# Expert layer of a decoder trunk: activations fetched by row transfers through slot tables in DRAM

## The chip, the cores and the metric

The kernel runs on one NeuronCore of one Trainium2 chip. The metric is the device time of one execution in microseconds (us), and for the kernel before it is 1563.54 us, the median of 3 runs that lie between 1563.01 and 1564.38 us. TensorE is called PE, VectorE DVE, ScalarE ACT, GpSimd Pool, and SP is the engine that issues the weight transfers. Everything is float32. A product of full precision is made of three TensorE products of rounded halves: each operand is split into a high part (rounded, made by ACT) and a low part (the rest, made by DVE).

## The reference, cut to what matters

A sequence of 16 meta tokens and 256 tokens of width 1024 passes two layers. The change touches the last part, the mixture of 8 experts of the second layer:

```python
logits = h @ w_router                                   # 256 tokens x 8 experts
top_val, top_idx = lax.top_k(logits, 2)
gates = softmax(top_val)                                # one weight per chosen expert
combine = sum(one_hot(top_idx, 8) * gates[..., None], axis=-2)
for e in range(8):
    y = y + combine[..., e:e+1] * ((silu(h @ w_gate[e]) * (h @ w_up[e])) @ w_down[e])
```

Here `h` is the normed residual, the three matrices of an expert are 1024 x 3584, 1024 x 3584 and 3584 x 1024, and the result is added to the residual.

## The kernel before, in words

Each expert works on up to 128 tokens, its slots. `pos` holds for each token and expert the slot that the token would have there, `sel` is 1 where the token chose the expert, `comb` holds the gates (lines 823 to 857 and 1028 to 1036). If an expert has more than 128 tokens, a loop under `tc.If(over == 1)` does the rest at the end; the data of these runs do not enter it.

**Gathering.** `gather` (L870) brings the activations of two experts together, as columns of a matrix `xh`, `xl` (high and low part, 1024 features by 2 x 128 slots). DVE builds a one-hot matrix `pg` from `pos` and `sel` (L875), and PE multiplies the token rows `h_hi` and `h_lo` by it: for each of 8 feature blocks 4 matmuls of 256 columns (L882), and 4 products of one column for the row scale `rsl`. ACT copies each block out of PSUM twice, into `xh` and `xl` (L883, L884). There is one buffer for `xh` and one for `xl`. The gather of pair 0 runs before the experts, and those of pairs 1, 2 and 3 are hung into the list of work near the end of experts 1, 3 and 5 (L1049).

**The expert loop.** `run` (L921) goes through a flat list of slabs. An expert has NJ = 7 steps j, and a step has three weight tiles of 2 MiB: gate, up and down. A tile is loaded by SP into one of 6 staging slots in turn (`wload`, L139 to L145; 5 in pool `wst`, 1 in `wst2`) and cut in two units of 2048 columns. A unit is split by ACT (`whi`, L163) and DVE (`wlo`, L164) into one of 3 buffers, and serves 12 matmuls of 512 columns. So a step has 72 such matmuls. Between them, 4 transposes turn the step's hidden activations (`turn_h`, L975), and the down product of a step follows the gate and up products of the next step. The products of `down` add up in two PSUM banks `dn` over all 7 steps.

**Scattering.** After an expert, `scatter` (L893), hung into step 1 of the next one (L1051), splits the two `dn` banks by ACT and DVE, turns the one-hot matrix by 2 transposes, multiplies by it in 8 matmuls of 512 columns (L907, L908) and adds 4 results, scaled by the gate, to the residual `acc` (L909). The last expert's `scatter` ends with the stores of the output.

**Order.** The program is written for a planner. It takes instructions in program order as priority, simulates the engines in time, and fixes each engine's order. `tc.high_priority(offset=PRI)` puts a block ahead by 300 places. A hook such as `hooks[e, "g", 1, 3]` runs a function behind a given slab: expert, which of gate, up, down, step, quarter of the tile.

**The dense layer.** The first layer's feed-forward (L581 to L625) is the place of one added part. There Pool multiplies `sg` by `rs` once for each of 28 blocks of 128 columns (L613), and DVE takes its result for the next product (L614). `psmm` has 4 PSUM banks in turn, and a block takes two of them. Just ahead of it Pool adds up the squares of 8 blocks (`sqa`, L193) while DVE makes the low parts `a_lo` (L199).

Of the kernel before, what the change touches and what calls it, by code (L numbers as in the profile page):

```python
# [18 lines left out]
P = 128  # L19
# [62 lines left out]
HIL = 3  # L82
UNIT = 2048

TCARGS = dict(schedule_with_timeline_sim=True)
# [13 lines left out]
def build(nc, tc, ctx, A, out, dbg=None, upto=None):  # L99
# [10 lines left out]
    hil = ch.enter_context(tc.tile_pool(name="hil", bufs=HIL))  # L110
    ps = ctx.enter_context(tc.tile_pool(name="ps", bufs=1, space=PSUM))

    def psmm():
# [5 lines left out]
    def pstr():  # L119
        return ps.tile([P, 512], F32, name="tr", bufs=2)  # L120
# [460 lines left out]
    with ExitStack() as c2:  # L581
        pf = c2.enter_context(tc.tile_pool(name="pf", bufs=2, reuse_waits="tile"))
        NJF = FF // 512

        def dense_down(j, fh, fl):
# [202 lines left out]
    acc = late.tile([P, 2, D], F32, name="acc")  # L788
    h_hi = late.tile([P, 2, D], F32R, name="h_hi")
    h_lo = late.tile([P, 2, D], F32R, name="h_lo")  # L790
    wst2 = ctx.enter_context(tc.tile_pool(name="wst2", bufs=WST2, side="right", reuse_waits="tile"))
    stage["pools"] = [wst] * WST + [wst2] * WST2
    cg_ = ctx.enter_context(ExitStack())
    hgp = cg_.enter_context(tc.tile_pool(name="hgp", bufs=1, side="right", reuse_waits="tile"))
# [38 lines left out]
    m8 = late.tile([P, 2, 8], F32, name="m8")  # L833
    m2 = hgp.tile([P, 2, 8], F32, name="m2")
    rep = hgp.tile([P, 2, NE], F32, name="rep")
    ex = late.tile([P, 2, NE], F32, name="ex")
# [29 lines left out]
    with ExitStack() as c4:  # L866
        pe = c4.enter_context(tc.tile_pool(name="pe", bufs=1, reuse_waits="tile"))
        wk = c4.enter_context(tc.tile_pool(name="wke", bufs=2, reuse_waits="tile"))

        def gather(es, xh, xl, pos=pos, sel=sel):  # L870

            pg = wk.tile([P, 2, 256], F32R, name="pg", bufs=2)
            for t in range(2):
                for i, e in enumerate(es):
                    nc.vector.tensor_scalar(pg[:, t, i * P:(i + 1) * P], iota, pos[:, t, e:e + 1],  # L875
                                            sel[:, t, e:e + 1], op0=OP.is_equal, op1=OP.mult)
            n = len(es) * P
# [12 lines left out]
            nc.vector.tensor_copy(r[:, :len(es)], o[:, :len(es)])  # L890
            return pg, r

        def scatter(e, col, yps, pg, comb=comb, post=None):  # L893

            y = stage["hil"].tile([P, UNIT], F32R, name="whi")
            yh, yl = y[:, 0:D], y[:, D:2 * D]
            pt = pstr()
            for t in range(2):
                tr(pt[:, t * P:(t + 1) * P], f(pg[:, t, col * P:(col + 1) * P]), P)
            pT = wk.tile([P, 256], F32R, name="pT2", bufs=1)  # L900
            nc.scalar.copy(pT, pt[:, :256])
            for n in range(2):
                sl = slice(n * 512, (n + 1) * 512)
                split_ps(yh[:, sl], yl[:, sl], yps[n])
                for t in range(2):
# [5 lines left out]
                    if post:  # L911
                        post(t, sl)

        def store(t, sl=slice(0, D)):
# [110 lines left out]

        gather_pair(0)

# [7 lines left out]
        for t in range(2):  # L1035
            nc.vector.tensor_scalar(comb[:, t], ex[:, t], dn[:, 1, t:t + 1], None, op0=OP.mult)
        o = psdn()
        mm(o[:, 0:NE], oneb, selb[:, 0], True, False)
# [3 lines left out]
        nc.vector.tensor_scalar(ovf, mx[:, 0:1], float(P), None, op0=OP.is_gt)  # L1042

        over = nc.values_load(ovf[0:1, 0:1], min_val=0, max_val=1)
# [12 lines left out]
        with tc.If(over == 1):  # L1057
# [6 lines left out]
            with tc.For_i(0, NE, 1) as e:  # L1064
                xh = wk.tile([P, KT, 256], F32R, name="xh", bufs=1)
                xl = wk.tile([P, KT, 256], F32R, name="xl", bufs=1)
                pg, r = gather((0,), xh, xl, cur[:, 0], cur[:, 1])
                ws = [w[bass.ds(e, 1)].rearrange("o a b -> (o a) b") for w in (WG, WU, WD)]
# [3 lines left out]
                run(more)  # L1072
                scatter(0, 0, st["y"], pg, cur[:, 2])
                nc.vector.tensor_copy(nxt[:, :, :, 0:NE - 1], cur[:, :, :, 1:NE])
# [26 lines left out]
```

## Time and profile before

| what | value |
|---|---|
| median of the runs (3 runs) | 1563.54 us |
| profiled execution, its own time | 1562.15 us |
| its span in the profile | 1560.4 us |
| PE busy | 1526.8 us, 98% |
| DVE busy | 1232.8 us, 79% |
| ACT busy | 1033.1 us, 66% |
| Pool busy | 118.3 us, 8% |
| moved by DMA | 433.70 MB, mean 278 GB/s |
| chain that ended last | PE 93%, ACT 3%, DVE 2% |

The span goes from the first to the last instruction, and the time of the execution is 1.75 us longer. Busy time counts each engine by itself; matmuls overlap in the pipeline, so the time from one matmul's start to the next one's is shorter than its duration. The chain of waits is followed back from the last instruction, and it is merged into pieces of one engine and line. The expert stage takes the last 1000 us, from about 559 us on.

### The profile page before, as it was taken

To read this page: it belongs to the slowest core of one execution; us is meant where nothing else is said; L and a number is where in the kernel's file an instruction comes from. 1 tells how busy PE (TensorE), PEld (TensorE's weight loads), DVE (VectorE), ACT (ScalarE), POOL (GpSimd) and SP (SyncE) were. 2 spreads that over 40 slices of the span, in tenths; PEclk is the share of its full clock that TensorE was granted. 3 is DMA by queue.
4 is the path that set the end of the run, shared out by engine and by line. 5 is a ranking of instruction groups with operands and counts; after the bars stand their busy time and mean duration, and the time that the engine had idled before them with its cause. 6 is when DMAs were issued, how large, how long until landed. Compare 5 with 4: busy or idle time off the path is not lost.

```text
span 1560.4 us, 21288 instructions
## 1 busy us (share of the span) xinstructions
PE 1526.8 (98%) x8558; PEld 1335.6 (86%) x8558; DVE 1232.8 (79%) x1248; ACT 1033.1 (66%) x1116; POOL 118.3 (8%) x146
## 2 busy tenths in 40 slices
PE   7989999999999989999999999999999999999997
PEld 7978999999999978888888888888888888888885
DVE  6875766666765678889879889879888888988986
ACT  5686644444545687767777777777777777777774
POOL 4431211112300100000000000000000000000000
PEclk9999999999999999999999999999999999999999
DMA  9521544443743659999999999998999998999980
GB/s 318 188 108 34 184 162 163 162 163 131 257 162 109 221 185 377 369 361 345 376 341 333 373 377 337 372 338 326 391 355 343 372 365 314 377 359 363 357 320 29
DMA packets 165822, 433.70 MB, mean 278 GB/s; under 512 B 5917, under 2 KB 10693, under 8 KB 158549
## 3 DMA queue, kind: packets, MB, share of 16 engines
q1 hardware_dynamic: 165652, 432.20, 75.4%
q8 instruction: 69, 1.13, 0.3%
q14 instruction: 37, 0.30, 0.1%
q10 hardware_dynamic: 64, 0.07, 0.0%
HBM read 431.21 MB, written 1.05 MB: 277 GB/s over the span
## 4 chain that ended last, share of the span: by engine, by line
PE 93%; ACT 3%; DVE 2%; issue 1%; DMA 0%; SPq 0%; DVEq 0%; ACTq 0%
PE mm L129 62%; PE dn L129 24%; PE tr L129 5%; PE tr L132 2%; ACT whi L163 1%; DVE wlo L164 1%; DMA w<-in_dsa_w_in_dram 0%; ACT kz L433 0%; DVE wlo L222 0%; ACT junk L298 0%; PE mm L132 0%; DVE sc L383 0%; ACT vz L475 0%; DVE acc L909 0%; DVE m L382 0%
## 5 line engine op out<-in xcount | busy, mean ns | idle before, releaser
L164 DVE TENSOR_TENSOR wlo<-w,whi 128x2048 fp32r<-128x2048 f32 (+1 forms) x473 | 930.4, 1981 | 179.0 <-ACT whi L163 177.5
L163 ACT CAST whi<-w 128x2048 fp32r<-128x2048 f32 (+1 forms) x473 | 781.5, 1658 | 401.9 <-PE mm L129 256.7
L129 PE MATMUL mm<-whi,xh 128*128 128x512 f32 x896 | 353.8, 395 | 1.2 <-ACT xl L884 1.0
L129 PE MATMUL mm<-wlo,xh 128*128 128x512 f32 x896 | 354.2, 397 | 0.4 <-DVE wlo L164 0.4
L129 PE MATMUL mm<-whi,xl 128*128 128x512 f32 x896 | 352.7, 394 | 0.0
L129 PEld LDWEIGHTS mm<-wlo,xh 128*128 128x128 f32 x896 | 169.1, 189 | 39.3 <-DVE wlo L164 3.6
L129 PE MATMUL mm<-a_hi,whi 128*128 128x272 f32 (+2 forms) x688 | 199.0, 291 | 2.8 <-ACT whi L221 1.4
L129 PEld LDWEIGHTS mm<-whi,xh 128*128 128x128 f32 x896 | 169.2, 189 | 37.3 <-ACT xl L884 1.2
L129 PEld LDWEIGHTS mm<-whi,xl 128*128 128x128 f32 x896 | 169.0, 189 | 37.1
L129 PE MATMUL mm<-a_hi,wlo 128*128 128x272 f32 (+2 forms) x688 | 198.7, 290 | 0.7 <-DVE wlo L164 0.7
L129 PE MATMUL mm<-a_lo,whi 128*128 128x272 f32 (+2 forms) x688 | 198.6, 289 | 0.0
L129 PE MATMUL dn<-whi,hTl 128*128 128x512 f32 x448 | 174.8, 391 | 1.4 <-DVE hTl L169 1.4
L129 PE MATMUL dn<-whi,hTh 128*128 128x512 f32 x448 | 174.3, 391 | 0.0
L129 PE MATMUL dn<-wlo,hTh 128*128 128x512 f32 x448 | 159.5, 396 | 0.3
L129 PEld LDWEIGHTS mm<-a_hi,whi 128*128 128x128 f32 (+1 forms) x688 | 128.5, 187 | 3.9 <-ACT whi L221 1.6
L129 PEld LDWEIGHTS mm<-a_hi,wlo 128*128 128x128 f32 (+1 forms) x688 | 128.4, 187 | 1.9 <-DVE wlo L164 0.9
L129 PEld LDWEIGHTS mm<-a_lo,whi 128*128 128x128 f32 (+1 forms) x688 | 128.7, 187 | 0.6
L129 PEld LDWEIGHTS dn<-whi,hTl 128*128 128x128 f32 x448 | 84.1, 188 | 20.0 <-DVE hTl L169 1.8
L129 PEld LDWEIGHTS dn<-whi,hTh 128*128 128x128 f32 x448 | 84.1, 188 | 18.3
L129 PEld LDWEIGHTS dn<-wlo,hTh 128*128 128x128 f32 x448 | 82.2, 188 | 19.3 <-DVE wlo L164 3.3
L129 PE MATMUL mm<-b_hi,whi 128*128 128x272 f32 (+1 forms) x264 | 75.1, 292 | 2.8 <-DVE gp L661 1.4
L129 PE MATMUL mm<-b_lo,whi 128*128 128x272 f32 (+1 forms) x264 | 75.8, 289 | 0.0
(350 smaller groups left out, 1676.1 us busy)
## 6 DMA issues: line engine op xcount, KB each, us to landing
w<-in_moe_w_gate_dram SPq DMA_DIRECT2D x56, 2048.0 KB, 10.1
w<-in_moe_w_up_dram SPq DMA_DIRECT2D x56, 2048.0 KB, 9.8
w<-in_moe_w_down_dram SPq DMA_DIRECT2D x56, 2048.0 KB, 9.0
w<-in_ffn_w_gate_dram SPq DMA_DIRECT2D x7, 2048.0 KB, 10.1
w<-in_ffn_w_up_dram SPq DMA_DIRECT2D x7, 2048.0 KB, 7.9
w<-in_ffn_w_down_dram SPq DMA_DIRECT2D x7, 2048.0 KB, 7.8
w<-in_mlstm_w_in_dram SPq DMA_DIRECT2D x6, 2048.0 KB, 10.3
w<-in_dsa_w_in_dram SPq DMA_DIRECT2D x4, 2048.0 KB, 10.2
```

The source lines that it names most:

```text
L129: nc.tensor.matmul(o, l, r, start=start, stop=stop)
L132: nc.tensor.transpose(o, i, ident[:k, :k])
L163: nc.scalar.copy(hr, src)
L164: nc.vector.tensor_tensor(lr, src, f(hr), OP.subtract)
```

## The change

- Two tables are set up in DRAM: `xs` with 256 rows for each expert (128 slots and 128 for the overflow), each a token's 1024 values, its row scale and 3 zeros (`DX` = 1028), and `ys` with 128 rows for each expert and one more row of zeros. At the start of the dense layer Pool clears a tile and issues 36 transfers that write zeros into them (16 halves of two columns for `xs`, 4 for `ys`).
- After the gates, about 26 small DVE operations work out for each token and each of its two experts the row numbers `idx` in both tables and the gate `gate2`. Pool adds `h_hi` and `h_lo` into a row tile `hrow`, which takes one of the staging slots of the weights, and issues 4 indirect transfers that write the rows into `xs`.
- Pairs 1 to 3 are no longer gathered by PE. In steps 1 and 3 of experts 1, 3 and 5 Pool issues a load of 128 rows of `xs` into a tile `row` (one buffer), and in steps 2 and 4 `turn_rows` turns it by 16 transposes for a pair and splits the result into a second pair of buffers `xh2`, `xl2` (pairs 1 and 3) or `xh`, `xl` (pair 2).
- Experts 0 to 6 are no longer scattered by PE: ACT copies the two `dn` banks into `row`, and Pool issues its store into `ys`. In steps 1 to 4 of expert 7 Pool issues 4 indirect loads of rows of `ys`, and DVE adds each, times its gate, to `acc`. Expert 7 is scattered as before, but its one-hot matrix is made and turned in its step 6.
- The gather of pair 0 is written inside `tc.high_priority(offset=PRI)`, and DVE instead of ACT copies its `xl`. The one-hot matrix has one buffer instead of two; `h_hi` and `h_lo` are freed after `hrow`, and `xh2`, `xl2` take their room.

The core of the diff; the code of the overflow loop, which does not run, is left out.

```diff
+    xs = dram.tile([NE * 2 * P, DX], F32, name="xs")
+    ys = dram.tile([NE * P + 1, D], F32, name="ys")
...
+        zero = pz.tile([P, DX // 2], F32, name="zero")
+        nc.gpsimd.memset(zero, 0.0)
+        for c in range(2):
+            for e in range(2 * NE):
+                nc.gpsimd.dma_start(xs[e * P:(e + 1) * P, c * DX // 2:(c + 1) * DX // 2], zero)
+            nc.gpsimd.dma_start(ys[(NE - 1) * P:NE * P, c * D // 2:(c + 1) * D // 2], zero[:, 0:D // 2])
+            nc.gpsimd.dma_start(ys[NE * P:NE * P + 1, c * D // 2:(c + 1) * D // 2], zero[0:1, 0:D // 2])
...
-                nc.scalar.copy(xl[:, kt, :n], o[:, 256:256 + n])
+                nc.vector.tensor_copy(xl[:, kt, :n], o[:, 256:256 + n])
...
+        def fetch(c, t):
+            held["y"] = r = row()
+            nc.gpsimd.indirect_dma_start(r[:, 0:D], None, ys[:, :],
+                                         bass.IndirectOffsetOnAxis(ap=idx[:, 1, c, t:t + 1], axis=0))
+
+        def add(c, t):
+            nc.vector.scalar_tensor_tensor(acc[:, t], held["y"][:, 0:D], gate2[:, c, t:t + 1], acc[:, t],
+                                           op0=OP.mult, op1=OP.add)
...
+        def load_rows(e):
+            held["r"] = r = row()
+            nc.gpsimd.dma_start(r, xs[e * 2 * P:e * 2 * P + P])
+
+        def turn_rows(r, xh, xl, rsl, col, q):
+            o = pstr()
+            for k in range(4):
+                tr(o[:, k * P:(k + 1) * P], r[:, (4 * q + k) * P:(4 * q + k + 1) * P], P)
+            dst = (slice(None), slice(4 * q, 4 * q + 4), slice(col * P, (col + 1) * P))
+            split_ps(xh[dst], xl[dst], o.rearrange("p (k s) -> p k s", k=4))
+            if q:
+                nc.scalar.copy(rsl[:, col:col + 1], r[:, D:D + 1])
...
+        def store_y(e, yps):
+            y = row()
+            for n in range(2):
+                nc.scalar.copy(y[:, n * 512:(n + 1) * 512], yps[n])
+            nc.gpsimd.dma_start(ys[e * P:(e + 1) * P], y[:, 0:D])
+
+        with tc.high_priority(offset=PRI):
+            gather_pair(0)
...
+        hrow = stage["pools"][stage["n"] % len(stage["pools"])].tile([P, 4096], F32, name="w")
+        stage["n"] += 1
+        hrow = hrow[:, 0:2 * DX].rearrange("p (t c) -> p t c", t=2)
+        nc.gpsimd.tensor_tensor(hrow[:, :, 0:D], f(h_hi), f(h_lo), OP.add)
+        nc.gpsimd.memset(hrow[:, :, D:DX], 0.0)
+        nc.gpsimd.tensor_copy(hrow[:, :, D], rt[:, 2:4])
+        for c in range(2):
+            for t in range(2):
+                nc.gpsimd.indirect_dma_start(xs[:, :], bass.IndirectOffsetOnAxis(ap=idx[:, 0, c, t:t + 1], axis=0),
+                                             hrow[:, t], None)
...
             if e % 2 and e + 1 < NE:
-                hooks[e, "d", NJ - 2, 0] = [lambda n=(e + 1) // 2: gather_pair(n)]
+                n = (e + 1) // 2
+                for col in range(2):
+                    j = 1 + 2 * col
+                    hooks.setdefault((e, "g", j, 0), []).extend(
+                        [lambda n=n: next_pair(n)] * (not col) + [lambda n=n, col=col: load_rows(2 * n + col)])
+                    for q in range(2):
+                        hooks[e, "gu"[q], j + 1, 1] = [lambda n=n, col=col, q=q: turn_rows(held["r"], *cur_x[n], col, q)]
             if e:
-                hooks[e, "g", 1, KT // 2 - 1] = [lambda e=e - 1: scatter(e, e % 2, es[e][-1]["y"], pgs[e // 2])]
+                hooks[e - 1, "d", NJ - 1, CF - 1] = [lambda e=e - 1: store_y(e, es[e][-1]["y"])]
+        parts = [(c, t) for c in range(2) for t in range(2)]
+        for k, (c, t) in enumerate(parts):
+            hooks[NE - 1, "g", 1 + k, 0] = [lambda c=c, t=t: fetch(c, t)]
+            hooks[NE - 1, "u", 1 + k, 3] = [lambda c=c, t=t: add(c, t)]
+        hooks[NE - 1, "g", NJ - 1, 0] = [last_hot]
...
-        scatter(NE - 1, 1, es[-1][-1]["y"], pgs[NE // 2 - 1], post=store)
+        scatter(NE - 1, es[-1][-1]["y"], hot["pT"], post=store)
```

## Rows read from the trace of the kernel before

**Rows 1.** The page, part 1: busy time, share of the span, instructions.

```profile
PE 1526.8 (98%) x8558; PEld 1335.6 (86%) x8558; DVE 1232.8 (79%) x1248; ACT 1033.1 (66%) x1116; POOL 118.3 (8%) x146
```

**Rows 2.** Busy time by stretch: four steps of expert 0, of expert 4, six of 2.

```profile
core 0: us, PE busy (x) PEld busy (x) DVE busy (x) ACT busy (x) POOL busy (x), PEclk, DMA share, GB/s
608.49:676.25 67.76, 67.76 (x306) 56.03 (x305) 59.69 (x33) 50.05 (x33) 0.00 (x0) 1.00 1.00 372
1119.63:1188.35 68.72, 68.72 (x307) 56.41 (x307) 58.60 (x33) 50.94 (x35) 0.00 (x0) 1.00 0.98 360
838.80:940.16 101.36, 101.36 (x457) 83.88 (x457) 90.07 (x49) 75.17 (x49) 0.00 (x0) 1.00 1.02 379
```

**Rows 3.** Chain of waits, expert stage: start us, length us, what, how many.

```profile
608.02 0.47 PE tr L132 x4
608.49 10.54 PE mm L129 x46
...
676.25 10.54 PE mm L129 x46
...
692.72 0.69 PE tr L132 x6
...
698.47 0.93 PE tr L129 x4
...
712.85 10.53 PE mm L129 x46
...
1456.59 10.53 PE mm L129 x46
```

**Rows 4.** Timeline of PE, end of the first gather: start us, duration us.

```profile
563.11 0.40 PE L129 MATMUL tr<-pg,h_hi 128*128 128x256 f32 x2
...
563.58 0.39 PE L129 MATMUL mm<-whi,xl 128*128 128x512 f32 x1
```

**Rows 5.** Groups by line on DVE, 608.49 to 676.25: busy us, mean ns, idle.

```profile
L164 DVE TENSOR_TENSOR wlo<-w,whi 128x2048 fp32r<-128x2048 f32 x25 | 57.3, 2291 | 8.4 <-ACT whi L163 8.4
L971 DVE SCALAR_TENSOR_TENSOR sg<-mm,rsl,sg 128x512 f32<-128x512 f32 x4 | 3.0, 746 | 0.0
L169 DVE TENSOR_TENSOR hTl<-tr,hTh 128x512 fp32r<-128x512 f32 x4 | 2.7, 685 | 0.0
```

**Rows 6.** Instructions on tile acc, 560 to 1530: duration ns min/median/max.

```profile
L909 DVE SCALAR_TENSOR_TENSOR acc<-tr,comb,acc x28: 739/743/752, 699.7 to 1447.8; 128x512 f32<-128x512 f32 x28
```

**Rows 7.** Timeline at the start of the expert stage: ACT, DVE, PE, DVE.

```profile
550.67 5.49 ACT L163 CAST whi<-w 128x2048 fp32r<-128x2048 f32 x3
552.76 6.68 DVE L164 TENSOR_TENSOR wlo<-w,whi 128x2048 fp32r<-128x2048 f32 x3
559.36 0.79 PE L129 MATMUL mm<-whi,xh 128*128 128x512 f32 x1 [0.98 <-ACT xl L884]
559.44 0.15 DVE L1032 TENSOR_TENSOR ex<-ex,sel 128x16 f32<-128x16 f32 x1
```

**Rows 8.** Durations ns min/median/max of DVE and Pool operations with two inputs.

```profile
L199 DVE SCALAR_TENSOR_TENSOR a_lo<-hT,gains,a_hi x8: 489/1012/1035, 153.2 to 168.1; 128x272 fp32r<-128x272 f32 x8
L613 POOL TENSOR_TENSOR sg<-sg,rs x28: 775/1485/1487, 178.3 to 394.4; 128x272 f32<-128x272 f32 x28
L193 POOL TENSOR_TENSOR sqa<-sqa,sq x7: 725/736/988, 528.3 to 547.1; 128x256 f32<-128x256 f32 x7
```

**Rows 9.** Timeline of Pool around the start of the dense layer.

```profile
139.53 0.53 POOL L543 COPY sm<-pb 128x128 f32<-128x128 f32 x2 [6.06 <-DVE pb L501]
...
189.05 1.48 POOL L613 TENSOR_TENSOR sg<-sg,rs 128x272 f32<-128x272 f32 x1 [4.56 <-ACT sg L610]
195.11 1.49 POOL L613 TENSOR_TENSOR sg<-sg,rs 128x272 f32<-128x272 f32 x1 [4.58 <-ACT sg L610]
```

**Rows 10.** Weight transfers: one issue on SP, and time to landing, 710 to 1500.

```profile
557.27 0.38 SPq L144 DMA_DIRECT2D w<-in_moe_w_up_dram  x1
...
DMA to landing us min/median/max: 7.5/9.9/11.3
```

More of the change, by code (lines that the diff above doesn't have):

```diff
@@ L788, in build @@
     acc = late.tile([P, 2, D], F32, name="acc")
-    h_hi = late.tile([P, 2, D], F32R, name="h_hi")
-    h_lo = late.tile([P, 2, D], F32R, name="h_lo")
     wst2 = ctx.enter_context(tc.tile_pool(name="wst2", bufs=WST2, side="right", reuse_waits="tile"))
     stage["pools"] = [wst] * WST + [wst2] * WST2
+    chl = ctx.enter_context(ExitStack())
+    hl = chl.enter_context(tc.tile_pool(name="hl", bufs=1, side="right", reuse_waits="tile"))
+    h_hi = hl.tile([P, 2, D], F32R, name="h_hi")
+    h_lo = hl.tile([P, 2, D], F32R, name="h_lo")
     cg_ = ctx.enter_context(ExitStack())
@@ L833, in build @@
     m8 = late.tile([P, 2, 8], F32, name="m8")
-    m2 = hgp.tile([P, 2, 8], F32, name="m2")
-    rep = hgp.tile([P, 2, NE], F32, name="rep")
+    m2 = late.tile([P, 2, 8], F32, name="m2")
+    rep = late.tile([P, 2, NE], F32, name="rep")
     ex = late.tile([P, 2, NE], F32, name="ex")
@@ L891, in gather, with turn_hot, scatter @@
             return pg, r
-        def scatter(e, col, yps, pg, comb=comb, post=None):
+        def turn_hot(pg):
+            pt = pstr()
+            for t in range(2):
+                tr(pt[:, t * P:(t + 1) * P], f(pg[:, t, 0:P]), P)
+            pT = wk.tile([P, 256], F32R, name="pT2", bufs=1)
+            nc.scalar.copy(pT, pt[:, :256])
+            return pT
+        def scatter(e, yps, pT, comb=comb, post=None):
             y = stage["hil"].tile([P, UNIT], F32R, name="whi")
             yh, yl = y[:, 0:D], y[:, D:2 * D]
[L897 to L901, printed above, removed]
             for n in range(2):
@@ L1036, in build @@
             nc.vector.tensor_scalar(comb[:, t], ex[:, t], dn[:, 1, t:t + 1], None, op0=OP.mult)
+        slot = late.tile([P, 2, NE], F32, name="slot")
+        fits = late.tile([P, 2, NE], F32, name="fits")
+        pick = late.tile([P, 2, NE], F32, name="pick")
+        selc = late.tile([P, 2, 2, NE], F32, name="selc")
+        idf = late.tile([P, 2, 2, 2], F32, name="idf")
+        idx = late.tile([P, 2, 2, 2], I32, name="idx")
+        gate2 = late.tile([P, 2, 2], F32, name="gate2")
+        nc.vector.memset(m2, -3.3e38)
@@ new lines, in build, with choose @@
+        nc.vector.tensor_copy(m2[:, :, 0:1], m8[:, :, 0:1])
+        for t in range(2):
+            nc.vector.match_replace(rep[:, t], m2[:, t], pl[t][:, 0:NE], SENT)
+        nc.vector.tensor_scalar(selc[:, 0], rep, -3.35e38, None, op0=OP.is_lt)
+        nc.vector.tensor_tensor(selc[:, 1], sel, selc[:, 0], OP.subtract)
+        nc.vector.tensor_scalar(fits, pos, float(P), None, op0=OP.is_lt)
+        def choose(dst, src):
+            for c in range(2):
+                nc.vector.tensor_tensor(pick, selc[:, c], src, OP.mult)
+                nc.vector.tensor_reduce(dst[:, c], pick, AX.X, OP.add)
@@ new lines, in build @@
+        for t in range(2):
+            nc.vector.scalar_tensor_tensor(slot[:, t], iota[:, 0:NE], float(2 * P), pos[:, t], op0=OP.mult, op1=OP.add)
+        choose(idf[:, 0], slot)
+        for t in range(2):
+            nc.vector.scalar_tensor_tensor(slot[:, t], iota[:, 0:NE], float(P), pos[:, t], op0=OP.mult, op1=OP.add)
+        nc.vector.scalar_tensor_tensor(slot, slot, float(-NE * P), fits, op0=OP.add, op1=OP.mult)
+        nc.vector.memset(slot[:, :, NE - 1:NE], 0.0)
+        choose(idf[:, 1], slot)
@@ L1037, in build @@
+        for c in range(2):
+            for t in range(2):
+                nc.gpsimd.indirect_dma_start(xs[:, :], bass.IndirectOffsetOnAxis(ap=idx[:, 0, c, t:t + 1], axis=0),
+                                             hrow[:, t], None)
+        chl.close()
+        x2 = ctx.enter_context(tc.tile_pool(name="x2", bufs=1, side="right", reuse_waits="tile"))
+        xb2 = [x2.tile([P, KT, 256], F32R, name=n) for n in ("xh2", "xl2")]
         o = psdn()
@@ L1066, in build @@
                 xl = wk.tile([P, KT, 256], F32R, name="xl", bufs=1)
-                pg, r = gather((0,), xh, xl, cur[:, 0], cur[:, 1])
+                r = wk.tile([P, 2], F32, name="rsl", bufs=2)
+                rw = row()
+                nc.sync.dma_start(rw, xs.rearrange("(e h p) c -> e h p c", h=2, p=P)[bass.ds(e, 1), 1]
+                                  .rearrange("o p c -> (o p) c"))
+                for q in range(2):
+                    turn_rows(rw, xh, xl, r, 0, q)
+                pg = onehot((0,), cur[:, 0], cur[:, 1])
                 ws = [w[bass.ds(e, 1)].rearrange("o a b -> (o a) b") for w in (WG, WU, WD)]
```

29 lines of the change are left out of this document (25 added, 4 removed).

## The prediction

> **What bounds the kernel now.** I read the busy shares first, then the stretches of the expert stage, then the chain of waits, and last the timelines at its start. TensorE (PE) is busy for 98% of the span, DVE 79%, ACT 66%, Pool 8% [rows 1]. In an undisturbed stretch of the expert stage PE is busy all the time at the full granted clock (1.00, the 2.4 GHz level), and DVE for 59.69 of 67.76 us [rows 2]. The chain shows why: it lies on PE alone and repeats. From 608.49 to 676.25 it takes 67.76 us for four steps, 16.94 us each: 46 matmuls in 10.54 us are 0.229 each, 72 are 16.47, and the four transposes of the hidden activations take 0.47 [rows 3]. So PE sets the end here, and what PE no longer issues is gained, if nothing else becomes late. Two others are close. The DMA engines' share is 1.00 at 372 GB/s in the same stretch, 1.02 at 379 GB/s in another [rows 2]; and DVE has six splits of 2.291, one product of 0.746 and one low part of 0.685 in a step, 15.2 of 16.94 us [rows 5].
>
> **The change part by part.**
>
> *Gathers and scatters taken from PE.* The same place in the pattern, the first full step behind a scatter, is reached at 712.85 and at 1456.59 [rows 3]. That is six experts, 743.74 us; 42 steps of 16.94 are 711.48; the excess, 32.3 us, is six scatters and all three later gathers. The seventh scatter lies between 676.25 and 712.85: 36.60 less two steps, 2.7. Together 35.0 us. By PE's own work: a scatter is two groups of four matmuls of 0.93 and two transposes, 0.69 − 0.47 = 0.22 [rows 3], so 2.08, seven make 14.6. A gather is 32 matmuls; four take 563.58 − 563.11 = 0.47 us [rows 4], so 3.76, with the products for the row scale at about 1 more, an estimate from the transposes' 0.12 each; three make 14.3. That is 28.9, and the other 6 us are short waits and steps that were a little longer. I take 32 as gone (from 28.9 to 35.0).
>
> *Transposes put on PE.* 3 pairs by 4 groups of four at 0.47 us [rows 3]: +5.6. Each group adds a split of 512 columns, 0.685 us, to DVE; in a step with two groups DVE has 15.2 + 1.4 = 16.6 us beside 16.94 + 0.94 = 17.9 on PE, so they stay hidden, though with little room. If each of the 12 groups waits 0.4 us for its rows or its bank, it is 10.4. I take 5.6.
>
> *Stores and fetches of results.* `store_y` gives ACT two copies where the scatter gave it two splits and a copy, and takes the splits and adds from DVE. The adds of the last expert are 1024 columns, by two of 0.743 us [rows 6] 1.5 us in each of four steps: DVE 16.7 beside 16.94. 0 on the path. The tail behind the last down product, a scatter and the output's stores, is as before; its one-hot work was not on the path. 0.
>
> *The start of the expert stage.* At 550.67 ACT takes three splits of weights, 5.49 us, before it empties the gather's banks, and PE's first expert matmul is at 559.36, behind ACT's `xl` copy [rows 7]. If the planner now places the gather's copies first, half of them on DVE, the first matmul can come some 4 us earlier. Against that, two things wait in front of DVE's first splits (552.76 to 559.4, rows 7): about 26 small operations at 0.15, 3.9 us, which stand ahead of the slabs in program order, and Pool's add of 2048 columns. Two-input operations of Pool and DVE hold each other up in this trace: Pool's product takes 0.775 at the least and 1.485 as a rule, which is when a DVE split runs, and DVE's `a_lo` goes from 0.489 to 1.012 beside Pool's `sqa` [rows 8]. Pool's 256 columns take 0.736 [rows 8], so 2048 take about 5.9, and a split that comes behind would wait that long. Behind the splits PE waits. So from −4 to +9; I take +1. The Trainium skill, "SBUF — State Buffer", section "Who interferes with whom", states the rule: a DVE instruction with two SBUF inputs and a GpSimd one that reads SBUF exclude each other, and the second to issue waits for the whole first. The rows above agree with it (1.485 for 0.775); by it alone, with Pool first, the start would cost +6 in place of +1, and the sum would be 5 us higher.
>
> *A staging slot for `hrow`.* It comes in turn ahead of the first expert weights, so five tiles are loaded ahead and not six; the sixth load waits until the four indirect writes have landed. Behind it on SP, in order, stands the load that was issued at 557.27 and all later ones, and the sixth tile is needed at about 585 (five tiles of 24 matmuls are 27.5 us from 559.36 on, and its split comes some 2 us ahead). `hrow` is ready at about 557 (some 551, when ACT turns to the weights [rows 7], and the 5.9 of the add); the four writes cover the same table, so each may wait for the one before; at 2 to 5 us each they end at 565 to 577. A load lands 9.9 us after its issue [rows 10], so the tile is there at 575 to 587. I take +2 (0 to +10); most of the cost is that the lead is smaller.
>
> *More bytes.* Between 712.85 and 1456.59 PE's time per pair falls to 237.2 + 1.9 (4 groups) = 239.1 us. In it go 42 weight tiles (88.1 MB), two stores and two row loads (2.1 MB): 90.2 MB, 377 GB/s. Shown as sustained are 372 over 68 us and 379 over 101 us [rows 2], with no growth of the wait to landing (11.3 at most). Six slots turn in two steps, 33.9 us; less 9.9 for landing and about 8 of use some 16 us of lead are left. At 377 nothing is lost; at 370 a pair takes 243.8, 4.7 more, 16 us over the stage, less what is left of the lead. I take +2 (0 to +12).
>
> *Zeros at the dense layer.* 36 issues on Pool, 8.9 MB at a time when transfers have room. Ahead of the products of the dense layer Pool is free from 139.5 [rows 9], when the attention's tiles that hold the new tile's room are about done, to 178.3 [rows 8], less 8 additions of about 1 us: 30 us. They stand ahead of the dense layer's products in program order, so those wait until all 36 are issued; DVE's next product and the PSUM bank wait for them. A block of the dense layer takes 195.11 − 189.05 = 6.06 us [rows 9], and PE can run some 9 us ahead in its four banks. So the stall is 36c − 39 us for a price c per issue. No row shows an issue by Pool: SP's takes 0.38 [rows 10], which makes 0; Pool's longest repeated operation, 1.485 [rows 8], makes 14. I take the nearer in kind, SP's, and allow three times that: 0 (0 to +14).
>
> *Sum.* −32 + 5.6 + 1 + 2 + 2 = −21.4. The profiled execution took 1562.15 us (span 1560.4 and 1.75 around it), so 1540.8; the median of the runs, 1563.54, is 1.4 above it: **1542 us**.
>
> **The rivals.**
>
> *Transfers become the bound, or the start eats the lead.* For it: the share is already 1.00 where nothing disturbs, and the breaks at the expert borders, in which the queue catches up, go. Against it: 379 GB/s over 101 us. If only the 360 GB/s of the third stretch [rows 2] were held, a pair would take 250.6, 11.5 more than PE, 40 us over three and a half pairs, less 16 of lead and the 2 in the sum; with half of that, or with a start at +9, the time is 1554. The Trainium skill, "DMA: Bandwidth & Descriptors", section "Where 436 GB/s comes from", says that the memory side holds a core to about 358 GB/s; the trace has 372 and 379, so the measurement decides against it here.
>
> *Rows come late, no change.* Load, transposes and result rows share one `row` buffer. If a load waits for the store before it and PE stands at each of the 12 groups of transposes for 1.8 us, that is 21 us, and the time is 1563. Against it: a step of 17 us lies between load and use, and a weight transfer of four times the size lands in 9.9.
>
> *Slower: Pool's zero transfers hold up the dense layer.* The stall 36c − 39 eats the gain from c = 1.68 us per issue. At 2.2 it is 40 us, and the time 1582. For it: Pool is an engine in order and 36 issues stand ahead of 28 products on which DVE and PE depend. Against it: it needs over four times SP's price.
>
> *The whole gain.* All 35.0 gone and a start 4 us earlier: −33, 1530. This is the lower end of the forecast's own range.
>
> **How the numbers follow.** The forecast, 1542 with its own range 1530 to 1552, has 0.58; the transfers or the start, about 1554 (up to 1560), 0.19; no change at 1563, 0.06; slower, about 1582, 0.15; below 1530, 0.02. The range 1530 to 1566 leaves out 0.02 and most of the slower case, and so holds 0.83. A measurement of this kernel tells about 0.2% from no change (1560.4 to 1566.7). Faster 0.79, same 0.06, slower 0.15.
>
> **What would show it.** In the profile after, `tr<-pg` and `tr<-whi,pT` matmuls should be left only at the first gather and the last scatter, 48 more transposes should stand in the chain, and the distance from one expert to the next should be about 118.6 us, 1.9 more per two. The first expert matmul should be near 559, with DVE's first split near it. A DMA share of 1.0 with PE waiting for `whi` would show the first rival; PE waiting for transposes of `row` the second; PE idle near 185 with Pool issuing transfers the third. I am wrong if the distance between experts is above 121 us, or if the dense layer shows a stall of over 10 us.

## The result, and the profile after

The changed kernel takes 1615.77 us, the median of 4 runs (1614.37 to 1617.39), against 1563.34 (1563.01 to 1564.38) for the kernel before beside it: a ratio of 1.0333 with a 95% interval of 1.032 to 1.0345. The forecast was 1542 and faster; it is 52 us slower. The profiled execution took 1617.39 us with a span of 1615.6, so 55.2 us of span have to be found.

Page part 1 of the kernel after, columns as in [rows 1]:

```profile
PE 1538.8 (95%) x8416; PEld 1327.2 (82%) x8416; DVE 1226.9 (76%) x1246; ACT 1025.3 (63%) x1071; POOL 169.2 (10%) x207
```

PE issues 142 matmuls fewer and yet is busy 12 us longer; idle time grew from 34 to 77 us. So two things were lost: PE stands still more, and its matmuls take longer. To find the places I read from PE's timeline when each expert's first gate matmul starts, and take distances (experts and their steps are counted from 0, and a step begins with its first gate matmul):

| stretch | before us | after us | difference |
|---|---|---|---|
| end of the dense layer | 547.89 | 561.84 | +13.95 |
| from there to expert 0 | 11.47 | 16.54 | +5.07 |
| expert 0 | 115.80 | 124.82 | +9.02 |
| experts 1, 3, 5 | 125.86, 126.22, 126.16 | 137.11, 133.53, 134.64 | +27.04 |
| experts 2, 4, 6 | 121.35, 122.22, 122.21 | 121.64, 121.38, 121.55 | −1.21 |
| expert 7 to its last matmuls | 129.33 | 131.35 | +2.02 |
| tail | | | −0.7 |

Both signs that the prediction named for being wrong are there: experts further apart than 121 us, and a stall of over 10 us in the dense layer. Windows of the kernel after at four of these places (columns as in [rows 2]):

```profile
180.00:190.00 10.00, 1.64 (x3) 0.89 (x4) 3.87 (x4) 5.94 (x10) 3.67 (x4) 0.59 0.63 219
190.00:200.00 10.00, 10.00 (x62) 10.00 (x61) 4.26 (x8) 3.89 (x7) 2.98 (x3) 0.73 0.12 28
...
650.00:660.00 10.00, 5.84 (x17) 4.06 (x16) 6.09 (x3) 6.07 (x4) 0.00 (x0) 0.83 0.97 373
...
766.20:795.00 28.80, 21.15 (x76) 15.77 (x76) 14.15 (x10) 12.72 (x12) 0.55 (x1) 0.82 0.61 229
...
860.00:940.00 80.00, 80.00 (x352) 64.78 (x351) 68.67 (x37) 58.35 (x38) 0.54 (x1) 1.00 1.00 367
```

Three of the four places hold idle PE, and there the granted clock is at the 1.2 GHz level for a part of the time (0.59 to 0.83 in the mean), and a pause costs more than its length: in the 10 us behind the first one PE is busy throughout and yet runs 62 matmuls, where the kernel before has 82 in the same stretch. The last one is undisturbed: PE busy throughout, clock 1.00. Even there 80 us hold 352 matmuls, 4.40 a microsecond, where [rows 2] has 306 in 67.76, 4.52.

**The dense layer.** Pool's timeline (start us, duration us, and in brackets the idle time ahead and what ended it):

```profile
142.71 9.00 POOL L594 DMA_DIRECT2D xs<-zero  x16 [0.31 <-POOL zero L591]
...
170.87 0.54 POOL L594 DMA_DIRECT2D xs<-zero  x1 [0.60 <-DMA xs<-zero]
...
175.60 0.85 POOL L197 TENSOR_TENSOR sqa<-sqa,sq 128x272 f32<-128x272 f32 x1
...
181.38 3.90 POOL L197 TENSOR_TENSOR sqa<-sqa,sq 128x272 f32<-128x272 f32 x4 [4.93 <-ACT sq L196]
```

An issue costs 0.56 us while nothing is in its way (16 in 9.00). Before eight of the last eleven Pool waits 0.6 to 0.9 us for an earlier zero transfer, and before one 3.2: some 9 us of waiting in all, and 33 us from the first issue to the end of the last, with two sums of squares and a wait for ACT between them. Five of the seven sums `sqa` come behind the issues. The last four wait 4.93 us more for ACT's squares, which stand behind ACT's weight splits in the written order. The chain of waits (start us, length us, what) goes through them and then through PE, at a granted clock of 0.73 in the mean of 190 to 200:

```profile
181.38 1.41 POOL sqa L197
...
187.17 1.86 DVE rs L209
189.64 15.44 PE mm L133 x100
```

**The start of the expert stage.** Timelines of Pool, DVE, ACT and PE, one line each:

```profile
564.39 4.62 POOL L1137 TENSOR_TENSOR w<-h_hi,h_lo 128x2048 f32<-128x2048 f32 x1 [2.64 <-DVE h_lo L173]
...
564.29 5.31 DVE L889 TENSOR_SCALAR pg<-c_iota,pos,sel 128x128 fp32r<-128x128 f32 x4
...
576.43 1.90 ACT L167 CAST whi<-w 128x2048 fp32r<-128x2048 f32 x1
...
578.38 0.79 PE L133 MATMUL mm<-whi,xh 128*128 128x512 f32 x1 [1.79 <-ACT whi L167]
```

DVE's four `pg` products took 1.11 us before; beside Pool's add they take 5.31, and the gather waits: the chain has them.

```profile
564.38 4.71 DVE pg L889 x2
```

Then ACT makes the first weight split only at 576.43, behind the copies of `xh`; in [rows 7] three splits were done ahead of them.

**Expert 0.** Two loads from SP's queue, two lines of ACT's timeline, and the chain:

```profile
629.62 0.37 SPq L148 DMA_DIRECT2D w<-in_moe_w_up_dram  x1
...
647.09 0.37 SPq L148 DMA_DIRECT2D w<-in_moe_w_gate_dram  x1
```

```profile
651.40 0.69 ACT L998 ACTIVATE sg<-mm,rsl 128x512 f32<-128x512 f32 x1 [5.01 <-PE mm L133]
651.99 5.49 ACT L167 CAST whi<-w 128x2048 fp32r<-128x2048 f32 x3
```

```profile
653.91 2.30 DVE wlo L168
656.26 4.62 PE mm L133 x12
```

Step 4 (from 645.52) takes 23.52 us where the steps around it take 17.3. The load into the slot that `hrow` had is issued at 647.09, the 13th load behind `hrow`'s add, but step 4 does not wait for it: it is the seventh gate load of the stage, so it brings the gate tile of step 6, which PE starts at 685.9. The up tile of step 4 is the fifth up load, issued at 629.62, and a load lands some 10 us after its issue. What the split at 651.99 waits for is its place in ACT's written order, behind `sg`, which waits 5.01 us for PE.

**A step without any disturbance.** Chain of the kernel after:

```profile
841.40 10.78 PE mm L133 x46
852.18 5.59 PE dn L133 x24
857.77 0.47 PE mm L133 x2
858.24 0.47 PE tr L136 x4
858.71 10.78 PE mm L133 x46
```

46 matmuls take 10.78 us, 0.234 each, where [rows 3] has 10.54, 0.229. A step is 17.31 in place of 16.94. Clock, shape and count are the same.

**Experts 1, 3 and 5.** Chain of the kernel after in expert 1 (step 4 starts at 768.14), and under it lines of Pool (the store, the two row loads) and of PE's timeline:

```profile
755.19 10.98 PE mm L133 x47
766.19 1.91 ACT whi L167
768.13 2.30 DVE wlo L168
770.47 4.22 PE mm L133 x9
774.72 1.91 ACT whi L167
776.65 2.30 DVE wlo L168
779.00 3.93 PE mm L133 x9
782.95 1.91 ACT whi L167
...
789.82 3.27 PE dn L133 x14
```

```profile
721.56 0.57 POOL L1088 DMA_DIRECT2D ys<-row  x1 [128.20 <-ACT row L1087]
727.66 0.57 POOL L1064 DMA_DIRECT2D row<-xs  x1 [5.53 <-PE mm L133]
...
776.92 0.55 POOL L1064 DMA_DIRECT2D row<-xs  x1 [48.68 <-ACT whi L167]
```

```profile
774.91 1.46 PE L136 MATMUL tr<-c_ident,row 128*128 128x128 f32 x8
```

Split, low part and matmuls run one behind the other, three times, as if only one of the three split buffers turned. The rows were not late. All row loads landed within 7.3 us, this one was issued at 727.66, and it is turned only at 774.91. It is the written order that has the eight transposes there. Their program place is step 2 of the expert; the planner put them into step 4, behind its first 12 matmuls, and around them the transposes of the hidden activations and the down slabs slipped behind the next gate slabs (from 755.19 to 789.82 the chain has no down product), whose splits then had no buffer.

### The profile page after: what moved, and what is told of

It reads as the page before. It is cut to its first block, busy times and chain, and to the rows that moved or that the text cites. A ratio compares the mean times of both kernels' runs of the same rounds, so it can differ in the third digit from the quotient of the medians.

```text
span 1615.6 us, 21080 instructions
## 1 busy us (share of the span) xinstructions
PE 1538.8 (95%) x8416; PEld 1327.2 (82%) x8416; DVE 1226.9 (76%) x1246; ACT 1025.3 (63%) x1071; POOL 169.2 (10%) x207
## 3 DMA queue, kind: packets, MB, share of 16 engines
q8 instruction: 68, 1.11, 0.3%
## 4 chain that ended last, share of the span: by engine, by line
PE 90%; DVE 4%; ACT 3%; issue 1%; DMA 0%; POOL 0%; SPq 0%; DVEq 0%; ACTq 0%; POOLq 0%
PE mm L133 61%; PE dn L133 24%; PE tr L133 3%; PE tr L136 2%; DVE wlo L168 2%; ACT whi L167 2%; DMA w<-in_dsa_w_in_dram 0%; ACT kz L437 0%; DVE wlo L226 0%; DVE pg L889 0%; PE mm L136 0%; POOL sqa L197 0%; ACT junk L302 0%; DVE sc L387 0%; DVE rs L209 0%
## 5 line engine op out<-in xcount | busy, mean ns | idle before, releaser
L133 PE MATMUL mm<-wlo,xh 128*128 128x512 f32 x896 | 361.7, 404 | 15.6 <-DVE wlo L168 15.6
L133 PE MATMUL mm<-whi,xh 128*128 128x512 f32 x896 | 360.8, 403 | 15.3 <-ACT whi L167 15.3
L133 PE MATMUL mm<-whi,xl 128*128 128x512 f32 x896 | 359.3, 401 | 0.0
L133 PE MATMUL dn<-whi,hTl 128*128 128x512 f32 x448 | 178.2, 398 | 3.7 <-DVE hTl L173 3.7
L133 PE MATMUL dn<-wlo,hTh 128*128 128x512 f32 x448 | 163.5, 400 | 0.0
L1088 POOL DMA_DIRECT2D ys<-row x7 | 3.8, 542 | 731.6 <-ACT row L1087 731.6
## 6 DMA issues: line engine op xcount, KB each, us to landing
w<-in_mlstm_w_in_dram SPq DMA_DIRECT2D x6, 2048.0 KB, 10.4
```

Source lines behind the costliest of these rows:

```text
L133: nc.tensor.matmul(o, l, r, start=start, stop=stop)
L1088: nc.gpsimd.dma_start(ys[e * P:(e + 1) * P], y[:, 0:D])
```

## The experiments

Three theories stood: **order** (the shared `row` buffer makes the planner displace slabs), **address** (the second pair of buffers moved other buffers in SBUF, and the distance between the stationary and the streamed operand sets the pace of matmuls), and **Pool** (zeros and `hrow`). The rival to the second was that the added transfers slow the matmuls; to the first, that rows are late.

### Address or traffic

96 unused bytes ahead of the split buffers in the kernel after, and 32 bytes in the kernel before, which has none of the added transfers; the order of all other instructions is the same.

```diff
         stage["hil"] = c4.enter_context(tc.tile_pool(name="hil2", bufs=HIL, reuse_waits="tile"))
+        nc.gpsimd.memset(stage["hil"].tile([P, 24], F32, name="pad", bufs=1), 0.0)   # e1; [P, 8] in e2
```

> The changed kernel with 96 unused bytes per partition ahead of the buffers of the split weight halves, so that they begin 96 bytes past a multiple of 128, as in the kernel before; in the changed kernel they begin on a multiple of 128. Nothing else differs, the order of instructions included. Theory (the matmul's time depends on where its streamed operand begins): the spacing of matmuls goes back from 0.234 to 0.229 us, a plain step from 17.3 to 16.94, some 53 steps by 0.34 = 18 us less: 1598. Rival (the wider spacing comes from more traffic in SBUF, transfers and the second buffer): 1616 as the changed kernel.

Measured (e1): 1606.48 us, 1.0276 (1.0259 to 1.0293), 9.3 less than after; half of what was expected. The chain has both values in one run, here a step with `xh2`, `xl2` and one with `xh`, `xl`:

```profile
856.85 10.45 PE mm L133 x46
...
1090.90 10.73 PE mm L133 x46
```

0.227 against 0.233 a matmul. The shift mended the pace with one pair of buffers only.

> The kernel before with 32 unused bytes ahead of the same buffers, so that they begin on a multiple of 128. It has none of the change's transfers. Theory (address): the spacing goes from 0.229 to 0.234 and a plain step from 16.94 to 17.3, some 50 steps by 0.34 = 17 us more: 1580. Rival (traffic): 1563, no change.

Measured (e2): 1578.47 us, 1.0096 (1.0079 to 1.0113). The kernel before, with nothing but a shift of 32 bytes, loses 15.4 us and has the pace of the kernel after:

```profile
845.88 10.73 PE mm L129 x46
856.61 5.60 PE dn L129 x24
```

So address, not traffic. Its experts 1 to 6 take 754.75 us for 744.02, which is what I count as the pace's share there: 10.7. Two more runs put all operands of the expert matmuls of the kernel before at the same place in a row of 512 bytes, once 96 bytes past a multiple of 512, once 0 (which also tells whether multiples of 64 are slow by themselves).

```diff
         wk = c4.enter_context(tc.tile_pool(name="wke", bufs=2, reuse_waits="tile"))
+        nc.gpsimd.memset(wk.tile([P, 16], F32, name="padx", bufs=1), 0.0)            # e8; [P, 120] in e11
...
         gather_pair(0)
+        nc.gpsimd.memset(wk.tile([P, 448 // 4], F32, name="padh", bufs=1), 0.0)
```

> The kernel before with nothing changed but where its buffers begin: activations, hidden activations and split halves all 96 bytes past a multiple of 512 (in the kernel before the activations begin at 32). Theory (the spacing of matmuls depends on where the stationary and the streamed operand lie to each other, and is least, 0.227, where both begin at the same place, as for the down products of the kernel before): gate and up matmuls go from 0.230 on the mean to 0.227, 2688 by 3.3 ns = 9 us less: 1554. Rival (only the streamed operand's place counts): 1563, no change.

Measured (e8): 1556.04 us, 0.9948 (0.9932 to 0.9965).

> The kernel before with activations, hidden activations and split halves all beginning on a multiple of 512 bytes (96 past it in the run of 1556 us). Theory (only the distance between the two operands of a matmul counts): spacing 0.227 and 1556 again. Rival (a streamed operand that begins on a multiple of 64 is slow by itself, as in the changed kernel): spacing 0.234, 1578 to 1582.

Measured (e11): 1556.12 us, 0.9954 (0.9937 to 0.9971). Chain of the second:

```profile
856.69 10.46 PE mm L129 x46
867.15 5.44 PE dn L129 x24
```

Both are the same, and 0.5% faster than the kernel before, whose own placing was not the best. Moving both operands together changes nothing (e8 against e11), moving one of them by 32 bytes does (e2 against the kernel before): what counts is where they lie to each other, not the place. In these two kernels, with both at the same place, the spacing is 0.227 to 0.228; in the others it lies between 0.227 and 0.234. Which distance gives which spacing, and why, is open.

### Order or late rows

First the rows are turned later, in steps 3 and 6, with the second load in step 4:

```diff
-                    j = 1 + 2 * col
+                    j = 1 + 3 * col
...
-                        hooks[e, "gu"[q], j + 1, 1] = [lambda n=n, col=col, q=q: turn_rows(held["r"], *cur_x[n], col, q)]
+                        hooks[e, "gu"[q], 3 + 3 * col, 1] = [lambda n=n, col=col, q=q: turn_rows(held["r"], *cur_x[n], col, q)]
```

> The changed kernel with the rows turned one step later (a load in step 1 and 4 of the odd experts, its transposes in step 3 and 6). In the order that comes out no weight slab stands out of turn on TensorE any more. Theory (the transposes are placed in the written order as if rows came some 40 us after their issue, they hold both banks for transposes, the hidden activations and the down slabs slip behind the next gate slabs, and the three buffers of split halves jam): odd experts fall from 134 to 137 to about 121.5, three times 13.7 = 41 us less: 1575. Rival (the rows are late on the chip itself, or the extra splits are what DVE has no room for): the waits move along with the transposes, 1605 to 1616.

Measured (e3): 1581.98 us, 1.0125 (1.0108 to 1.0142), 33.8 less than after. Experts 1, 3 and 5 take 124.10, 124.17 and 123.55, and no slab is displaced. This leaves open whether the buffer is the cause, so the store of results gets a buffer of its own and everything else stays, the places of the loads and turns too:

```diff
         def store_y(e, yps):
-            y = row()
+            y = wk.tile([P, D], F32, name="yrow", bufs=1)
...
-            cur = pe.tile([P, 3, 2, NE], F32, name="cur")
+            cur = wr.rearrange("p k e -> p (k e)")[:, 0:6 * NE].rearrange("p (i t e) -> p i t e", i=3, t=2)
```

(The second edit only makes room; it is in the overflow loop.)

> The changed kernel with a second staging row: the stores of results have a buffer of their own, the loads of rows keep `row`. Nothing else differs in the source (the loads and transposes stay where they were); in the order that comes out no weight slab is displaced and the transposes stand 1.5 to 2 steps earlier. Theory (the one buffer makes each load wait for the store ahead of it, the written order allows for that wait at its own price, and the late place of the transposes jams the split halves): odd experts 123.5 in place of 134 to 137, 33 to 36 us less: 1580. Rival (it was the moving of the transposes by a step that helped in the run with rows turned later, not when the rows come): odd experts stay above 130, 1605 to 1616.

Measured (e9): 1574.37 us, 1.0077 (1.006 to 1.0094), 41.4 less than after. The same stretch of expert 1, windows:

```profile
735.00:790.00 55.00, 55.00 (x250) 44.67 (x249) 48.12 (x29) 40.19 (x29) 1.09 (x2) 1.00 1.00 371
```

PE is busy for all of the 55 us at clock 1.00; experts 1, 3 and 5 take 123.14, 122.62 and 122.67, together 368.43 for 405.28. The pace of the matmuls is that of the kernel after (0.233). So 36.85 us hang on one buffer shared by a store and a load. What in the planner's own reckoning makes it displace the slabs was not looked into. The even experts, without loads and transposes, take 362.73 together, so these cost 5.7 when nothing is displaced.

### Zeros

The same bytes in 8 issues, of which four cover eight blocks of 128 rows each:

```diff
-            for e in range(2 * NE):
-                nc.gpsimd.dma_start(xs[e * P:(e + 1) * P, c * DX // 2:(c + 1) * DX // 2], zero)
+            for g in range(2):
+                nc.gpsimd.dma_start(xs[g * NE * P:(g + 1) * NE * P, c * DX // 2:(c + 1) * DX // 2]
+                                    .rearrange("(e p) c -> p e c", p=P), zero.unsqueeze(1).to_broadcast([P, NE, DX // 2]))
```

> The changed kernel with the zeros written by 8 transfers in place of 36 (each source row read eight times over), the same bytes at the same place. Theory (Pool's issues and its waits between them delay the sums of squares, and PE stands 10 us and runs at half clock behind it): the stall goes, 10 to 14 us less: 1602 to 1606. Rival (8.9 MB of writes at 385 to 399 GB/s hold up the weights of the dense layer): the stall stays, 1616.

Measured (e4): 1603.70 us, 1.0266 (1.0249 to 1.0283), 12.1 less than after. Windows of this kernel where the kernel after stood still, and ahead of it:

```profile
160.00:170.00 10.00, 10.00 (x81) 10.00 (x81) 7.68 (x10) 6.31 (x10) 3.81 (x4) 1.00 1.03 414
...
180.00:190.00 10.00, 10.00 (x81) 10.00 (x81) 7.18 (x11) 4.64 (x7) 2.56 (x2) 1.00 0.79 282
```

The same bytes go at up to 414 GB/s, and PE doesn't stop. The 36 issues were the cause, with Pool's time and the order that comes with them, and not the bytes.

### The slot of `hrow`, and Pool's add

`hrow` takes the `row` buffer, half of the tokens at a time; in a second run it also waits for `pg`:

```diff
-        hrow = stage["pools"][stage["n"] % len(stage["pools"])].tile([P, 4096], F32, name="w")
...
+        for t in range(2):
+            hrow = row()
+            nc.vector.tensor_copy(hrow[:, 0:1], f(pgs[0][:, 1, 255:256]))            # e6 alone
+            nc.gpsimd.tensor_tensor(hrow[:, 0:D], f(h_hi[:, t]), f(h_lo[:, t]), OP.add)
```

> The changed kernel with the slot rows put together in the `row` tile, one half of the tokens after the other, in place of a staging slot of the weights; otherwise the same work. Theory (the slot stays out of the weights' rotation until the written order lets a load into it behind thirteen others, so that load is late for step 4 of expert 0, 23.5 us in place of 17.3, and the start loses its lead): the stall goes, 6 us, and 2 to 4 at the start: 1606 to 1608. Rival (at this rate the transfers have no lead to give, whatever the slot): the stall comes back at another step, 1613 to 1616.

Measured (e5): 1605.51 us, 1.0267 (1.025 to 1.0284), 10.3 less than after. Expert 0 takes 116.82 for 124.82, its step 4 17.17 for 23.52. So the slot was the cause, but not by a late load, as the theory has it: in e5 two splits stand ahead of step 4's `sg` again (643.70 and 646.50, `sg` at 648.31). The edit was not as clean as it looks: it also moved buffers, and a step's 24 down products take 5.50 us for 5.60, some 0.7 of the 8.0 in expert 0 and of the gain in every other expert. The start is not shorter: 16.34 us for 16.54.

> As the run before, and Pool's additions of the slot rows made to wait for DVE's four one-hot products of the first gather. Theory (Pool's addition of 2048 columns, 4.62 us, holds DVE's products up, 5.31 in place of 1.1 us): 4 us less than the run before. Rival (Pool then holds up DVE's first splits instead, by the same time): 0 to 1 us less.

Measured (e6): 1605.77 us, 1.027 (1.0253 to 1.0287): no gain. The timelines of Pool and DVE:

```profile
563.96 2.39 POOL L1137 TENSOR_TENSOR row<-h_hi,h_lo 128x1024 f32<-128x1024 f32 x1
...
562.35 1.11 DVE L889 TENSOR_SCALAR pg<-c_iota,pos,sel 128x128 fp32r<-128x128 f32 x4
...
564.60 3.90 DVE L168 TENSOR_TENSOR wlo<-w,whi 128x2048 fp32r<-128x2048 f32 x1
```

`pg` has its 1.11 us, but it had 1.10 in e5 already, where Pool's add held up a small copy (1.85 us for 0.16), so the 4 us were not there to gain. Now DVE's first split takes 3.90 in place of 2.28. The block moved to what came next. And the start is as long as ever, 16.53 us: in e5 and e6 ACT has its three first splits ahead of the gather again, and the chain, here that of e5, goes through DVE's three splits to the copies of `xl` that stand behind them:

```profile
569.66 2.20 DVE wlo L168
...
572.02 0.34 DVE xl L903
```

### All of it, and what is left

The edits of e3, e4 and e6, and pads that put all operands 96 bytes past a multiple of 512:

```diff
+        nc.gpsimd.memset(wk.tile([P, 16], F32, name="padx", bufs=1), 0.0)
...
+        nc.gpsimd.memset(x2.tile([P, 96], F32, name="pad2", bufs=1), 0.0)
...
+        nc.gpsimd.memset(wk.tile([P, 104], F32, name="padh", bufs=1), 0.0)
```

> The changed kernel with all of it: rows turned a step later, zeros in 8 issues, slot rows in the `row` tile behind the one-hot products, and the split halves, the activations of both buffers and the hidden activations all beginning 96 bytes past a multiple of 512. Theory (the stalls and the spacing were what ate the gain, and gathers and scatters off PE are worth some 30 us): 1616 less 34, 12, 9 and 4, less 56 steps by 0.4 for a spacing of 0.227 to 0.229 (some 22): 1530 to 1540, faster than before. Rival (with PE that fast the transfers bound: 377 GB/s and more are wanted a pair): 1545 to 1560, with the DMA share at 1.0 and PE waiting for whi.

Measured (e7): 1540.04 us, 0.9852 (0.9835 to 0.9868). Windows of 80 us in expert 0 and of 40 in expert 3:

```profile
600.00:680.00 80.00, 80.00 (x362) 66.42 (x361) 71.15 (x40) 59.34 (x38) 0.00 (x0) 1.00 1.02 382
...
945.00:985.00 40.00, 40.00 (x182) 33.20 (x181) 34.10 (x19) 30.24 (x20) 0.54 (x1) 1.00 1.03 398
```

PE is always busy at 382 and 398 GB/s, with the share at 1.02 and 1.03. Still left were the first matmul at 564.18 (560.56 in e8) and the last expert. So ACT copies `xl` again, as before the change, and the four fetches go into the `xh` and `xl` buffers, free by then, so that none waits for another:

```diff
-                nc.vector.tensor_copy(xl[:, kt, :n], o[:, 256:256 + n])
+                nc.scalar.copy(xl[:, kt, :n], o[:, 256:256 + n])
...
-            held["y"] = r = row()
+            if t == 0:
+                w_ = wk.tile([P, KT, 256], F32R, name=("xh", "xl")[c], bufs=1)
+                held["y", c] = f(w_.rearrange("p k s -> p (k s)"))
+            r = held["y", c][:, t * D:(t + 1) * D]
```

> The mended kernel of 1540 us with two more edits: both halves of the first gather copied by ACT again, as in the kernel before, and the four fetches of results put into the activations' buffer that is free in the last two experts, so that no fetch waits for an add. Theory (the half copied by DVE stands behind its three first splits and costs the start 3.6 us; the last add holds up the last hidden activation by 3.2; expert 1 loses some 4 to an order that is better here): 1529 to 1532. Rival (DVE has no room for four adds of 1.28 us whenever they come): the end keeps its 25.3 us step and the time is 1533 to 1537.

Measured (e10): 1535.01 us, 0.9824 (0.9808 to 0.9841), the best of all, but in the rival's range. The first matmul comes at 560.26, and the start falls from 16.60 us to 13.12, as the theory had it; expert 1 takes 121.74 for 124.19. The fetches did not pay: the last step falls from 25.26 to 23.97, but the adds now come together in DVE, step 4 of expert 7 grows by 2.55, and that expert takes 127.80 for 126.54.

The last run prices the scatters by themselves: e10 with PE's scatters again, and no stores, fetches and adds.

```diff
-                hooks[e - 1, "d", NJ - 1, CF - 1] = [lambda e=e - 1: store_y(e, es[e][-1]["y"])]
...
+                hooks[e, "g", 1, KT // 2 - 1] = [lambda e=e - 1: scatter(e, es[e][-1]["y"], turn_hot(onehot((e,))))]
```

> As e10, but results are added up by scatters on TensorE after each expert, as in the kernel before, without stores, fetches and adds; rows are still gathered by transfer. Theory (a scatter costs PE some 2.7 us, the two steps around it being 36.4 in place of 33.7 in the kernel before with its buffers moved): seven are 19 us, so 19 above e10, some 1549. Rival (stores and fetches cost about as much in waits, and the gathers were all of the gain): within 5 us of e10.

Measured (e12): 1547.25 us, 0.99 (0.9883 to 0.9916), 12.2 more than e10, between the two. Experts 1 to 6 take 729.56 in place of 717.93, so a scatter is worth 1.94. Against e8, whose operands have the same distance, these six experts (738.93) give the gathers: 9.4 for three, 3.1 net of their transposes, and 5.0 with the 1.9 of those.

## Why the prediction was wrong

**What bounds the kernel** was right: PE, and whatever makes it wait. By terms:

| step of the prediction | taken (bounds) | measured | shown by |
|---|---|---|---|
| gathers and scatters removed | −32 (−28.9 to −35.0) | −26.6 in experts 1 to 6, which have six of the seven scatters | e8, e10, e12 |
| transposes put on PE | +5.6 (to +10.4) | 5.7 by themselves; the order that they come with +36.85 | e9, e3 |
| stores, fetches, adds, tail | 0 | +1.8 in expert 7 (127.80 against 127.97 with a scatter of 1.94), tail −0.7 | e10, e12, the table above |
| start | +1 (−4 to +9) | +5.07; +1.6 with `xl` copied by ACT | the table above, e10 |
| slot for `hrow` | +2 (0 to +10) | +8.0, some 0.7 of it pace | e5 |
| more bytes | +2 (0 to +12) | 0 | e7 |
| zeros | 0 (0 to +14) | +13.95 | e4 |
| pace of the matmuls left on PE | no term | +10.7 in experts 1 to 6 | e1, e2, e8, e11 |

The parts of experts 1 to 6 (+25.83) go together as 10.7 + 36.85 − 21.7; the last is what remains, and e10 against e8 gives −21.0 directly (717.93 for 738.93). It fits the removal of 26.8 by PE's own work in six scatters and three gathers (12.5 + 14.3), less 5.6 for the transposes. So of the two ends of that term, the own work was right; the excess of 32.3 in [rows 3] held some 5 us of waits that stay.

**The step that failed first** is the one for the transposes: "If each of the 12 groups waits 0.4 us for its rows or its bank, it is 10.4." The rival on late rows named the right resource, "Load, transposes and result rows share one `row` buffer", and then priced it as waits on the chip. But rows land in 3.6 to 7.3 us. What cost 36.85 us is that the planner, which fixes each engine's order beforehand, moved other work because of that buffer. An edit has two prices, its own and that of the order it brings about, and the second had no term.

**The step that wasn't there** is the pace. The sum took 42 steps of 16.94 as given, since nothing in them was edited. But `xh2`, `xl2` and the freed tiles moved buffers in SBUF, and the steps became longer, by 0.37 us at most, and by 0.25 (10.7 over 42) on the mean in e2. No range and no rival had this, nor the displaced order, so even the slowest case on record, 1582, is 34 us short.

**Zeros**: the mechanism was written down as a rival, and both its numbers were off. The price came from SP's issues (0.38); Pool's took 0.54 to 0.56 each, and 33 us in all with the waits and sums between them. By "36c − 39" that would still be no stall; but the 39 us of cover weren't there. They took the products of the blocks for the first to wait, while the `sqa` sums stand ahead of these, behind the issues, and `rs`, which every block needs, behind the sums, as the chain shows.

**`hrow`**: the term waited for a late reload of the slot, taken as the sixth load. The reload came much later, as the 13th load behind `hrow`'s add, and nothing waited for it. The 6.4 us in step 4 are again a price of the order: ACT's splits stand behind `sg`. Why the planner put them there was not looked into.

**Start**: Pool's add and DVE did hold each other up, 4.62 us for the 5.9 estimated, but it caught `pg`, ahead of the gather, and not the splits. That this is what the start costs is not shown: in e5, e6 and e7 `pg` has its 1.1 us and the start still takes 16.34 to 16.60. What shortened it by 3.5 was giving the copies of `xl` back to ACT (e10). The prediction had counted these copies on DVE as a help, toward its −4. The Trainium skill, "SBUF — State Buffer", section "Who interferes with whom", has a DVE instruction with two SBUF inputs and a GpSimd one that reads SBUF exclude each other. e6's split has two such inputs and agrees, 3.90 for 2.28. `pg` has one SBUF tensor beside its scalars, so it is not a case of that sentence, and that the +6 lies near the 5.07 is luck.

**Bytes**: transfers are not the bound, as weighed. The 358 GB/s of "DMA: Bandwidth & Descriptors" in the Trainium skill, section "Where 436 GB/s comes from", is again exceeded, by 398 over 40 us.

The size of the gain was about right. With order, addresses, zeros, slot and fetches mended the change gives 1535.01. Beside e8, the kernel before at the same pace, that is 21.0 us less, and the sum was −21.4. But this is another kernel than the one that was to be predicted, and the agreement is partly luck: the sum had −26.4 for gathers, scatters and transposes and +5 around them, the runs have −21.0 in experts 1 to 6 and little around them.

## What to carry to other kernels

When an edit makes two uses share one buffer in a kernel whose order is planned (a store and a load, or a staging slot lent to other data), compare the written orders before pricing waits: work that was not touched may have moved. When an edit adds or frees a tile, compare the addresses of the operands of the matmuls that stay, since a pace that "nothing changed" can change by 3%. And cost transfers issued by a computing engine as time of that engine, with the waits between them.

## What was unexpected of the hardware

- Matmuls of 512 columns from full buffers at clock 1.00 are 0.227 us apart when stationary and streamed operand begin at the same place modulo 512 bytes (e8, e11), and up to 0.234 apart in other kernels of the same order and shapes. In this kernel that is worth 8 us one way (e8, e11) and 15 the other (e2).
- 36 plain transfers issued by Pool took 33 us from first to last, 0.54 to 0.56 us an issue and 0.6 to 0.9 of waiting for an earlier transfer before eight of the last eleven; the same bytes in 8 issues left PE undisturbed.
- One core's transfers ran at 398 GB/s over 40 us and at 414 over 10 us beside a PE that was always busy.
